# Projecting the keys' latent, v and part of c_q as seven products of halved matrices

## The chip, the cores and the metric

One core of a Trainium2 chip runs the whole kernel as one program. The metric is the device time of one execution in microseconds (us), median of several runs. The engines are named as in the profile: PE is TensorE's matrix multiply and PEld its weight load, DVE is VectorE, ACT is ScalarE, POOL is GpSimd, and SP is SyncE, which here only issues DMA transfers, in the order of its queue.

## The reference

One layer of a decoder, 1024 tokens of 1024 features in float32: a feed-forward half step, a mixer with three branches, a second feed-forward half step. The change lies in the mixer's input projection and in what follows it.

```python
h = rmsnorm(x, mix_norm)
z = h @ w_in       # columns: u 512 | v 512 | c_q 384 | c_kv 256 | k_rope 32 | q_mem 512 | gates 3 x 1024
u, v = gelu(z_u), gelu(z_v)
y_a = u * (tril(w_s) @ layernorm(v) + b)                       # 128-token chunks, 8 groups
q  = rope(rmsnorm(rmsnorm(c_q)  @ w_uq))                        # 8 heads of 64 + 32
kv = rmsnorm(c_kv) @ w_ukv                                     # 8 heads of 64 + 64
k  = rope(rmsnorm([kv_nope, k_rope]))
y_b = causal_attention(q, k, kv_v)
y_c = attention(rmsnorm(q_mem), memory of 256 tokens)          # k and v of the memory from mem_w_kv
x  = x + (sum_i sigmoid(gate_i) * (y_i @ w_branch_i)) @ w_out
```

## The kernel before

Every operand of a product is kept as two tiles, `hi` (a cast on ACT) and `lo` (the rest, a subtraction on DVE); the function `split` makes both, and `mm3` multiplies with three matmuls per 128 rows of the contraction (hi by hi, hi by lo, lo by hi). So one 128 x 128 block against 512 columns is three matmuls of 512 columns.

Most of the work is done in units of the class `Seven` (feed-forward) and its child `Gates`: a unit makes two 128-feature rows of outputs for all 1024 tokens from four halves of a matrix in seven products of half size, with additions on DVE before and after, as in Strassen's method. A unit is 7 products x 4 blocks x 3 = 84 matmuls of 512 columns. `Gates.run` goes through a list of units (gates, the memory queries, u), in an order of PE written by hand; outputs go to DRAM (`gate0`, `gate1`, ...).

After the last unit comes `mixer`, whose order on the engines is made by a scheduler at build time:

- `latent` projects c_q feature by feature (3 blocks x 2 halves of the tokens x 8 x 3 = 144 matmuls of 512 columns) and c_kv with the rotary key token tile by token tile (`zrow`, 8 tiles x 8 x 3 = 192 matmuls of 288 columns), takes the sums of squares, normalizes c_kv and transposes it.
- `qkv` makes q, k and v of the heads for two token tiles at a time: per tile two banks of 384 columns (9 matmuls each) and one pair of 512 (12 matmuls). ACT copies them out and squares them, DVE sums the squares (L516, L528), takes the inverse roots in a chain of small instructions, and scales q (L541) and k (L543, L545); POOL rotates q (L359 to L364); SP stores v, k and q to DRAM (`vd`, `kd`, `qd`). The tiles q and k have two buffers, v has one.
- `sgu` projects v in `gelu_rows` (192 matmuls of 512 columns), normalizes it (L646 to L652), splits it into v_hi and v_lo, and mixes it over the tokens of a chunk (`mix(0)` and `mix(1)`, one for each half of the tokens: 8 groups of 3 matmuls of 256 columns, eight ACT evictions with a bias into the tile u, 16 transposes of u, four DVE products with the gate u). Among these stands `mem_kv`, keys and values of the memory (two products of 48 matmuls of 512 columns), whose weights come from DRAM as `wkv` (already split).
- then the three branches with their attention.

The pool of `sgu` takes the memory that the pool of `qkv` had.

Of the kernel before, what the change touches and what calls it, by code (L numbers as in the profile page):

```python
# [8 lines left out]
F32 = mybir.dt.float32  # L9
# [32 lines left out]
ZB = ZU + SGW // P  # L42
# [4 lines left out]
class Kernel:  # L47
# [181 lines left out]
    def latent_gains(self, const):  # L229
        nc, a = self.nc, self.a  # L230
        self.g_ckv = self.bcast_row(const, "g_ckv", a["mla_ckv_norm"], KVR)

# [183 lines left out]
    def zrow(self, ps, h, i, w):  # L416

        c = slice(i % 4 * P, i % 4 * P + P)
        for d in range(DT):
            self.mm3(ps, tuple(x[:, c] for x in h[i // 4][d]), w[d], d == 0, d == DT - 1)  # L420

    def to_feature(self, dst, srcs, gain=None):

        nc = self.nc
        b = self.bank()
# [9 lines left out]
    def latent(self, h):  # L435
# [4 lines left out]
        cq = [self.split_pair() for _ in range(QR // P)]  # L440
        ckv = [self.split_pair() for _ in range(KVR // P)]
        kr, krs, krr, eps = (self.lp.tile(s, F32, name=n) for s, n in (
            ([P, NT, ROPE], "kr"), ([P, NT], "krs"), ([P, NT, ROPE], "krr"), ([P, NT], "eps")))
        w = self.convert(self.w_cq)

        def c_q(hf):
            acc, cols = None, slice(hf * 512, hf * 512 + 512)
            for j, d in enumerate(cq):
                b = self.bank()
                for k in range(DT):  # L450
                    self.mm3(b, w[j * DT + k], h[hf][k], k == 0, k == DT - 1)
                acc = self.norm_feed(acc, b, 512)
                self.split_gain(d[0][:, cols], d[1][:, cols], b, self.g_cq[:, j:j + 1])
            nc.vector.tensor_scalar(
                eps[:, hf * 4:hf * 4 + 4], self.token_sums(acc), EPS / QR, EPS * EPS, op0=ALU.mult, op1=ALU.add)

        n, width = a["w_ckv"].shape[-1], KVR
        with tc.tile_pool(name="lat", bufs=1) as p:
            wkv = self.load(
                a["w_ckv"], lambda: [p.tile([P, 3 * n], F32R, name=x, bufs=3) for x in ("kvhi", "kvlo")])  # L460
            for hf in (1, 0):
                c_q(hf)
                xs = []
                for j in range(2):
                    pm = self.mm() if j == 0 else None
                    ss = self.stat("l_ss", 2)
                    for k in range(2):
                        i = hf * 4 + j * 2 + k
                        ps = pm[:, k] if pm is not None else self.bank()
                        self.zrow(ps[:, :n], h, i, wkv)  # L470
                        x = p.tile([P, n], F32, name="l_xs", bufs=6)
                        sq = p.tile([P, n], BF16, name="l_junk", bufs=2)
                        nc.scalar.activation(sq[:, :width], ps[:, :width], ACT.Square, accum_out=ss[:, k:k + 1])
                        nc.scalar.copy(x, ps[:, :n])
                        nc.scalar.activation(sq[:, width:], x[:, width:], ACT.Square, accum_out=krs[:, i:i + 1])
                        nc.scalar.copy(kr[:, i], x[:, width:])
                        xs.append(x)
                    r = self.rms(ss, 2, width)
                    for k, x in enumerate(xs[-2:]):
                        nc.vector.scalar_tensor_tensor(  # L480
                            x[:, :width], in0=x[:, :width], scalar=r[:, k:k + 1], in1=self.g_ckv,
# [1588 lines left out]
```

## Time and profile before

| what | value |
|---|---|
| median of 3 runs | 2186.36 us (2186.1 to 2187.63) |
| profiled execution | 2187.86 us, its span 2186.1 us |
| granted clock over the span | 0.998 |
| PE busy | 2171.8 us, 99% of the span |
| DVE, ACT, POOL busy | 1559.3, 907.0, 268.9 us |

The span is the time from the first to the last instruction that the profiler saw. A busy PE is one with a matmul in flight: the engine can be busy without a pause and still run a matmul slowly if its clock is lowered. The granted clock says how far it was: 1.00 is 2.4 GHz and 0.50 is 1.2 GHz.

### The profile page before, as it was taken

How to read it: one execution, taken by the hardware profiler on the slowest of the kernel's cores; microseconds unless marked ns; L12 is line 12 of the kernel's file. 1: busy time of each engine (PE TensorE's matmuls, PEld its weight loads, DVE VectorE, ACT ScalarE, POOL GpSimd, SP SyncE). 2: the span in 40 equal slices, each digit the busy share in tenths (PEclk: the TensorE clock that was granted, in tenths of full speed). 3: DMA queues.
4: the chain of work that ended last, by engine and by line, in shares of the span. 5: the costliest groups of instructions: out<-in, count | busy, mean ns of one | idle time of the engine just before them, and what ended most of it. 6: DMA issues, size and time to landing. Idle time of an engine off the chain costs nothing.

```text
span 2186.1 us, 27650 instructions
## 1 busy us (share of the span) xinstructions
PE 2171.8 (99%) x10258; PEld 1813.6 (83%) x10258; DVE 1559.3 (71%) x2384; ACT 907.0 (41%) x1490; POOL 268.9 (12%) x269
## 2 busy tenths in 40 slices
PE   9999999999999999999999999999999999999999
PEld 5888888888887888889888889988888888888887
DVE  7976666679889656653876679885886666667884
ACT  5433333343445434443535469833432322234332
POOL 3011111100000000000311321140011211210000
PEclk9999999999999999999999999999999999999999
DMA  4253444385433444532495631093033223337443
GB/s 146 83 192 140 145 140 154 137 316 173 130 116 105 146 167 168 176 108 73 161 311 198 247 144 59 14 355 133 30 141 97 98 98 101 116 124 295 169 130 106
DMA packets 123927, 324.72 MB, mean 149 GB/s; under 512 B 14608, under 2 KB 22928, under 8 KB 123792
## 3 DMA queue, kind: packets, MB, share of 16 engines
q1 hardware_dynamic: 123792, 322.96, 42.3%
q8 instruction: 80, 1.31, 0.2%
q14 instruction: 55, 0.45, 0.1%
HBM read 221.72 MB, written 101.19 MB: 148 GB/s over the span
## 4 chain that ended last, share of the span: by engine, by line
PE 92%; DVE 4%; ACT 1%; DMA 1%; issue 1%; POOL 1%; SPq 0%; ACTq 0%; POOLq 0%
PE one L148 14%; PE one L150 14%; PE one L149 14%; PE bank L148 13%; PE bank L149 13%; PE bank L150 13%; PE mm L148 2%; PE mm L149 2%; PE mm L150 2%; PE bank L989 1%; PE bank L1004 1%; DMA w<-in_ffn_w_gu_dram 1%; PE bank L1005 1%; PE bank L428 1%; DVE wlo L137 1%
## 5 line engine op out<-in xcount | busy, mean ns | idle before, releaser
L136 ACT CAST whi<-x 128x1024 fp32r<-128x1024 f32 (+1 forms) x201 | 191.4, 954 | 443.8 <-PE one L149 168.7
L1390 DVE TENSOR_TENSOR t<-t,one 128x512 f32<-128x512 f32 x186 | 127.7, 687 | 214.6 <-PE one L150 214.5
L137 DVE TENSOR_TENSOR wlo<-x,whi 128x1024 fp32r<-128x1024 f32 (+1 forms) x201 | 243.5, 1213 | 34.3 <-ACT whi L136 24.7
L148 PE MATMUL bank<-h,whi 128*128 128x512 f32 x676 | 263.4, 390 | 0.0
L149 PE MATMUL bank<-h,whi 128*128 128x512 f32 x676 | 263.1, 389 | 0.0
L150 PE MATMUL bank<-h,wlo 128*128 128x512 f32 x676 | 263.0, 389 | 0.0
L148 PE MATMUL one<-h,whi 128*128 128x512 f32 x508 | 199.6, 393 | 0.0
L149 PE MATMUL one<-h,whi 128*128 128x512 f32 x508 | 198.4, 391 | 0.0
L150 PE MATMUL one<-h,wlo 128*128 128x512 f32 x508 | 198.4, 391 | 0.0
L148 PE MATMUL one<-w,whi 128*128 128x512 f32 x424 | 165.4, 390 | 0.1
L150 PE MATMUL one<-w,wlo 128*128 128x512 f32 x424 | 165.0, 389 | 0.0
L149 PE MATMUL one<-w,whi 128*128 128x512 f32 x424 | 165.0, 389 | 0.0
L1812 POOL TENSOR_TENSOR raw<-raw 128x512 f32<-128x512 f32 x38 | 57.0, 1501 | 800.3 <-DVE raw L1667 713.7
L131 ACT CAST whi<-w 128x1024 fp32r<-128x1024 f32 (+1 forms) x108 | 95.1, 899 | 143.4 <-PE one L149 55.2
L132 DVE TENSOR_TENSOR wlo<-w,whi 128x1024 fp32r<-128x1024 f32 (+1 forms) x108 | 110.1, 1033 | 60.8 <-ACT whi L131 60.7
L150 PEld LDWEIGHTS bank<-h,wlo 128*128 128x128 f32 x676 | 126.9, 188 | 26.4
L149 PEld LDWEIGHTS bank<-h,whi 128*128 128x128 f32 x676 | 126.9, 188 | 26.2
L148 PEld LDWEIGHTS bank<-h,whi 128*128 128x128 f32 x676 | 126.9, 188 | 26.0
L148 PE MATMUL bank<-whi 128*128 128x512 f32 x352 | 136.9, 389 | 0.0
L149 PE MATMUL bank<-wlo,whi 128*128 128x512 f32 x352 | 136.9, 389 | 0.0
L150 PE MATMUL bank<-whi,wlo 128*128 128x512 f32 x352 | 136.9, 389 | 0.0
L149 PEld LDWEIGHTS one<-h,whi 128*128 128x128 f32 x508 | 96.0, 189 | 20.0 <-issue 0.2
(391 smaller groups left out, 4895.6 us busy)
## 6 DMA issues: line engine op xcount, KB each, us to landing
x<-in_ffn_w_gu_dram SPq DMA_DIRECT2D x78, 512.0 KB, 4.9
w<-tdt SPq DMA_DIRECT2D x40, 512.0 KB, 4.3
tdb<-raw SPq DMA_DIRECT2D x64, 256.0 KB, 2.1
h<-in_ffn_w_down_dram SPq DMA_DIRECT2D x64, 256.0 KB, 6.0
gate<-raw SPq DMA_DIRECT2D x31, 512.0 KB, 2.8
w<-tdb SPq DMA_DIRECT2D x30, 512.0 KB, 4.7
tdt<-w SPq DMA_DIRECT2D x48, 256.0 KB, 2.1
x<-in_w_gate_dram SPq DMA_DIRECT2D x21, 512.0 KB, 6.4
```

The lines of the kernel that those rows point to most:

```text
L131: self.nc.scalar.copy(hi, src)
L132: return (eng or self.nc.vector).tensor_tensor(lo, src, hi.bitcast(F32), op=ALU.subtract)
L136: self.nc.scalar.copy(hi, src)
L137: return lambda: self.nc.vector.tensor_tensor(lo, src, hi.bitcast(F32), op=ALU.subtract)
L148: i = mmul(out, s[0], m[0], start=first, stop=False, **kw)
L149: mmul(out, s[0], m[1], start=False, stop=False, **kw)
L150: self.last = mmul(out, s[1], m[0], start=False, stop=last, **kw)
L428: nc.tensor.transpose(b[:m, k * P:(k + 1) * P], s, self.ident)
L989: nc.tensor.transpose(b[:, at:at + P], prs[t][:, kk * P:(kk + 1) * P], self.ident)
L1004: nc.tensor.matmul(o, w, pt[0], start=n == 0, stop=False)
L1390: return self.nc.vector.tensor_tensor(out, x, y, op=ALU.add)
L1812: sub = lambda d, x, y: (eng or nc.gpsimd).tensor_tensor(d, x, y, op=ALU.subtract)
```

## The change

One unit more is put among the gates' units (`ZC // 2`, ninth in the list). It makes 256 of the 384 columns of c_q and stores them as `gate32` and `gate33`; `parts` splits them with their gain into the DRAM tensor `cq`, and `latent_squares` and `latent_sums` make the sums of squares. The remaining 128 columns of c_q, c_kv, the rotary key and v (416 + 512 = 928 columns) are projected in `token_rows`, which stands behind the last unit in the same hand-written order of PE. Both the 928 columns and the 1024 tokens and the 1024 features are halved, and the 2 x 2 x 2 blocks are multiplied in seven products; the tokens' combinations are those that the units already had (`norm.op`), and those of the weights are made by `both` on DVE. A product is 4 token tiles x 4 blocks of the contraction x 3 = 48 matmuls of 464 columns, so there are 336.

`latent`, `zrow` and `gelu_rows` fall away, and with them the second loading and normalization of a half of x that `Gates.run` did for them. The new class `Latents` normalizes c_kv (`norm`), loads the c_q of DRAM back (`load`), and transposes c_kv and the last 128 columns of c_q (`turn`). v's layer normalization moves: for the first half of the tokens it stands in `qkv`, as `asides` between the pairs of token tiles; for the second half it stands behind `mem_kv`'s first product. `sgu` begins with the splits of v and `mem_kv`; half of the first product's weights are loaded ahead, into tiles of the x4 pool.

```diff
@@ run
-            r0 = self.const.tile([P, 4], F32, name="r0")
-            gates.run(x1d, r0)
+            latents = gates.run()
...
-            merged = self.mixer(norm)
+            merged = self.mixer(latents)
@@ Gates.run
-        units = [3, 4, ZQ // 2, 5, 6, ZQ // 2 + 1, *range(7, ZQ // 2), ZU // 2, ZU // 2 + 1]
+        units = [3, 4, ZQ // 2, 5, 6, ZQ // 2 + 1, 7, 8, ZC // 2, *range(9, ZQ // 2), ZU // 2, ZU // 2 + 1]
-                    k.w_cq = list(k.fetch(k.a["w_cq"], [x4, x4]))
-                    for p in range(2):
-                        norm.t.t[0, p] = w4()
-                        self.nc.sync.dma_start(norm.t.t[0, p], x1d[0, p])
-                    norm.s[0] = k.norm_scale(r0)
-                    for p in range(2):
-                        norm.norm(0, p)
+                last = f == units[-1]
+                if last:
+                    self.row_weights(range(5), [w4, x4, x4, x4, x4])
...
+            return self.token_rows()
@@ token_rows
+        def product(out, w, name, first=False, ps=range(2)):
+            for p in ps:
+                for t in range(4):
+                    for i in range(2):
+                        s = tuple(x[:, i, t * P:(t + 1) * P] for x in norm.op[name][p])
+                        k.mm3(out[t][:, :RW], s, w[2 * p + i], first and p + i == 0, p + i == 2, skip_group_check=True)
...
+        product(x, w, "t2", True)
+        w = ready(A12)
+        both(A12, A12, S2, ALU.subtract)
+        v1, _ = room(w4)
+        for t in range(4):
+            tt(v1[t], p1[t], x[t][:, :RW], op=ALU.add)
+        both(A21, A21, A22, ALU.add)
+        product(a, w, "b21")
...
+        product(y, w, "t4", ps=(1,))
+        for t in range(4):
+            tt(v1[t], v1[t], y[t][:, :RW], op=ALU.add)
+            gelu(1, t, v1[t], False)
+        return lat
@@ qkv
                     nc.sync.dma_start(d, q[:, t].rearrange("p (g x) d -> p g (x d)", x=2))
+                next(asides, None)
@@ sgu
-            take(0)
-            mt = self.mem_rows()
-            take(1)
+            split(0)
+            kv = self.mem_kv(self.mem_t, self.mem_w)
+            next(kv)
+            for v in rows[1]:
+                self.layer_norm(v)
+            split(1)
             nc.scalar.activation(self.stat("warm", 1), vs[1][0][:, 3, SGW - 1:].bitcast(F32), ACT.Exp, scale=0.0)
             mix(0)
@@ mixer
-        with tc.tile_pool(name="lt", bufs=1) as self.lp:
-            self.latent_gains(self.lp)
-            self.qkv(*self.latent(h))
+        def asides():
+            lat.turn(0)
+            self.mem_w = self.mem_weights(0, [self.split_pair] * 2)
+            yield
+            self.mem_t = self.mem_rows()
+            self.layer_norm(lat.v[0][0])
+            yield
+            self.layer_norm(lat.v[0][1])
+            yield
```

**PE behind qkv.** Before, the last matmuls of `qkv` (into mm_8566, with halves of the transposed c_kv in x4 tiles) are followed by the first of the 192 for v (into bank_8835 and bank_8836, one bank for each token tile, with the normalized h in h4 tiles):

```order
L148 MATMUL mm_8566<-whi_8098,x4_7460 128x512
L149 MATMUL mm_8566<-wlo_8099,x4_7460 128x512
L150 MATMUL mm_8566<-whi_8098,x4_7461 128x512
L148 MATMUL bank_8835<-whi_8637,h4_5214 128x512
L148 MATMUL bank_8836<-whi_8637,h4_5214 128x512
L149 MATMUL bank_8835<-wlo_8638,h4_5214 128x512
```

Now `qkv` ends with mm_8795, and `mem_kv`'s first product begins (mm_8878), with weights that were loaded ahead (x4_8400, x4_8401) and the memory's rows (h4_8536, h4_8537):

```order
L151 MATMUL mm_8795<-whi_8242,h4_8114 128x512
L152 MATMUL mm_8795<-wlo_8243,h4_8114 128x512
L153 MATMUL mm_8795<-whi_8242,h4_8115 128x512
L151 MATMUL mm_8878<-x4_8400,h4_8536 128x512
L152 MATMUL mm_8878<-x4_8401,h4_8536 128x512
L153 MATMUL mm_8878<-x4_8400,h4_8537 128x512
```

When `mem_kv`'s 96 matmuls are through (the last of them into mm_9119), the first of `mix(0)` follow, which need v_hi_8860 and v_lo_8861:

```order
L151 MATMUL mm_9119<-whi_8964,h4_8538 128x512
L152 MATMUL mm_9119<-wlo_8965,h4_8538 128x512
L153 MATMUL mm_9119<-whi_8964,h4_8539 128x512
L151 MATMUL bank_9033<-v_hi_8860,x4_8856 128x256
L151 MATMUL bank_9038<-v_hi_8860,x4_8856 128x256
L151 MATMUL bank_9043<-v_hi_8860,x4_8856 128x256
L151 MATMUL bank_9048<-v_hi_8860,x4_8856 128x256
```

The matmuls of v have gone from behind `qkv`, and `mix(0)`, between whose groups matmuls of `mem_kv` stood before, now stands behind the last of these by itself.

**ACT behind qkv.** Now, behind `qkv`'s last evictions (L462 to L464) and those of `mem_kv`'s first product (L624, L625), the casts of v for both halves come (h_7967 and h_7968 are the first), then the load of an activation table (L603), and then the eight evictions of `mix(0)` (L587):

```order
L624 ACTIVATE t<-mm 128x512
L625 COPY h_8927<-mm 128x512
L624 ACTIVATE t<-mm 128x512
L625 COPY h_8927<-mm 128x512
L134 CAST whi<-raw 128x512 x4
L134 CAST v_hi<-h_7967 128x1024
L134 CAST v_hi<-h_7968 128x1024
L134 CAST v_hi<-h_7794 128x1024
L134 CAST v_hi<-h_7795 128x1024
L603 ACT_TABLE_LOAD
L603 ACTIVATE warm<-v_hi 128x1
L587 ACTIVATE u<-bank,c_sg_b 128x4x64 x8
```

Before, the order behind `qkv`'s last evictions was the Gelu of the first half of v (L610) and two casts:

```order
L525 ACTIVATE sq<-mm 128x512
L526 COPY k<-mm 128x8x64
L527 COPY v<-mm 128x512
L610 ACTIVATE x_8669<-mm 128x1024
L610 ACTIVATE x_8670<-mm 128x1024
L131 CAST v_hi<-x_8669 128x1024
L131 CAST v_hi<-x_8670 128x1024
L610 ACTIVATE h_8833<-bank 128x512 x2
L610 ACTIVATE h_8834<-bank 128x512 x2
```

The first two casts write tiles that lie in memory of the pool of `qkv`, and in the new order they wait for the stores of its last k and q (`kd`, `qd`).

**DVE at the beginning of qkv.** Before, the sums of squares (tile qk_ss) followed the last subtraction for the transposed c_kv at once:

```order
L132 TENSOR_TENSOR x_7459<-bank,x_7458 128x512
L132 TENSOR_TENSOR x_7461<-bank,x_7460 128x512
L516 TENSOR_REDUCE qk_ss<-sq 128x8
L534 TENSOR_SCALAR qk_v<-qk_ss,eps 128x8
L528 TENSOR_REDUCE qk_ss<-sq 128x8
L529 TENSOR_SCALAR qk_ss<-qk_ss,krs 128x8
```

Now statistics and first steps of v's normalization (L551, L552, L555; h_7794 and h_7795 are rows of v) and subtractions for weights stand among the first of them:

```order
L135 TENSOR_TENSOR wlo<-raw,whi 128x512 x2
L551 BN_STATS bn<-h_7794 128x6
L551 BN_STATS bn<-h_7795 128x6
L552 BN_AGGR mv<-bn 128x2
L551 BN_STATS bn<-h_7795 128x6
L453 TENSOR_REDUCE qk_ss<-sq 128x8
L552 BN_AGGR mv<-bn 128x2 x2
L555 SCALAR_TENSOR_TENSOR h_7794<-h_7794,mv,h_8139 128x512
L552 BN_AGGR mv<-bn 128x2
```

The scheduler has moved the normalization of the first rows of v ahead of the place that the code gives it.

## Rows read from the trace of the kernel before

**Rows 1.** The page: each engine's busy time, share of the span and instructions.

```profile
PE 2171.8 (99%) x10258; PEld 1813.6 (83%) x10258; DVE 1559.3 (71%) x2384; ACT 907.0 (41%) x1490; POOL 268.9 (12%) x269
```

**Rows 2.** PE's waits: who waited for whom, total us, times, longest.

```profile
PE bank L384 <- POOL t L1235: 2.6, 1, 2.6
...
PE bank L148 <- DVE x L132: 1.3, 1, 1.3
```

**Rows 3.** Windows: length, busy time of each engine, clock, DMA share, GB/s.

```profile
840.00:940.00 100.00, 100.00 (x460) 83.30 (x459) 60.38 (x96) 40.76 (x51) 2.96 (x3) 1.00 0.48 163
1020.00:1040.00 20.00, 19.71 (x129) 18.47 (x127) 8.06 (x29) 5.71 (x23) 1.73 (x6) 1.00 0.16 54
1040.00:1050.00 10.00, 9.00 (x48) 8.53 (x49) 6.40 (x15) 8.58 (x20) 0.00 (x0) 1.00 0.05 21
1041.00:1098.00 57.00, 57.00 (x279) 50.81 (x280) 48.88 (x94) 30.05 (x65) 20.68 (x20) 1.00 0.55 184
1087.00:1150.00 63.00, 63.00 (x301) 52.86 (x300) 46.50 (x121) 20.48 (x36) 8.69 (x9) 1.00 0.91 310
1150.00:1160.00 10.00, 9.54 (x66) 8.56 (x64) 7.56 (x12) 7.55 (x15) 0.00 (x0) 1.00 0.86 331
```

**Rows 4.** Timeline of PE: start, length, instruction, at three places.

```profile
985.55 0.30 PE L148 MATMUL mm<-kvhi,h 128*128 128x288 f32 x1
...
989.52 0.29 PE L148 MATMUL mm<-kvhi,h 128*128 128x288 f32 x1
...
1050.14 0.33 PE L148 MATMUL bank<-whi,x 128*128 128x384 f32 x1
...
1053.28 0.39 PE L148 MATMUL mm<-whi,x 128*128 128x512 f32 x1
...
1085.56 0.39 PE L148 MATMUL mm<-whi,h 128*128 128x512 f32 x1
...
1087.15 0.39 PE L148 MATMUL bank<-whi,h 128*128 128x512 f32 x1
```

**Rows 5.** Groups of DVE by shape, 1041 to 1160: busy us, mean ns.

```profile
L132 DVE TENSOR_TENSOR wlo<-raw,whi 128x512 fp32r<-128x512 f32 x12 | 10.0, 860 | 0.0
...
L671 DVE TENSOR_TENSOR t<-t,bank 128x512 f32<-128x512 f32 x8 | 5.1, 681 | 1.4 <-PE bank L670 1.4
...
L646 DVE BATCH_NORM_STATS2 bn<-x 128x6 f32<-128x512 f32 x4 | 2.6, 686 | 8.4 <-ACT x L610 8.4
```

**Rows 6.** Timelines of DVE, SP and ACT: the end of qkv, and v.

```profile
1094.08 1.76 DVE L541 TENSOR_TENSOR q<-q,rs_y 128x1536 f32<-128x1536 f32 x1
...
1101.67 1.10 SPq L553 DMA_DIRECT2D qd<-q  x2
...
1118.80 2.74 DVE L652 SCALAR_TENSOR_TENSOR x<-x,rs_y,ln_b 128x512 f32<-128x512 f32 x4
...
1120.37 1.06 ACT L131 CAST v_hi<-x 128x1024 fp32r<-128x1024 f32 x1 [12.50 <-DMA wlo<-wkv]
```

**Rows 7.** DMA issues, 1040 to 1180: times, KB each, median us to landing.

```profile
qd<-q SPq DMA_DIRECT2D x8, 384.0 KB, 3.5
...
h<-mrows SPq DMA_DIRECT2D x4, 512.0 KB, 7.0
```

**Rows 8.** Timelines of PE and ACT and ACT's groups: transposes of k, mix(1).

```profile
1149.64 1.03 PE L428 MATMUL bank<-ident,h 128*128 128x128 f32 x8
1150.43 0.36 PE L148 MATMUL bank<-v_hi,x 128*128 128x256 f32 x1
...
1156.58 0.48 PE L148 MATMUL bank<-x,whi 128*128 128x512 f32 x1
...
1152.33 3.05 ACT L664 ACTIVATE u<-bank,c_sg_b 128x256 f32<-128x256 f32 x8
...
L677 ACT ACT_TABLE_LOAD x1 | 1.3, 1283 | 0.0
```

**Rows 9.** Window behind PE's longest wait, columns as in rows 3.

```profile
39.00:46.00 7.00, 6.95 (x23) 5.84 (x24) 5.22 (x15) 1.04 (x1) 0.00 (x0) 0.55 0.00 0
```

More of the change, by code (lines that the diff above doesn't have):

```diff
@@ L413, in norm_put, with to_feature @@
         self.split(hi, lo, x)
[L416 to L422, printed above, removed]
+    def to_feature(self, dst, srcs, gain=None, bank=None):
         nc = self.nc
-        b = self.bank()
+        b = (bank or self.bank)()
         m = srcs[0].shape[-1]
@@ L433, in to_feature, with qkv @@
             self.split_gain(dst[0], dst[1], v, gain)
-    def latent(self, h):
+    def qkv(self, lat, asides):
         nc, a, tc = self.nc, self.a, self.tc
         half = ROPE // 2
[L440 to L481, printed above, removed]
-                            op0=ALU.mult, op1=ALU.mult)
-                for c, d in enumerate(ckv):
-                    self.to_feature(
-                        tuple(t[:, hf * 512:hf * 512 + 512] for t in d),
-                        [x[:, c * P:(c + 1) * P] for x in xs])
-                t = slice(hf * 4, hf * 4 + 4)
-                self.rotate(
-                    nc.gpsimd, p, krr[:, t], kr[:, t], [x[:, t] for x in self.rope["k"]], [P, NT // 2, half])
-        return cq, ckv, krr, krs, eps
@@ L492, in qkv @@
-    def qkv(self, cq, ckv, krr, krs, eps):
-        nc, a, tc = self.nc, self.a, self.tc
-        half = ROPE // 2
+        cq, krr, krs, eps = lat.cq, lat.krr, lat.krs, lat.eps
         wq = self.load(a["mla_w_uq"])
@@ L785, in query_roots, with latent_squares, latent_sums @@
         nc.gpsimd.tensor_scalar(self.mq_nr[:, :, c], self.mq_r[:, :, c], -1.0, None, op0=ALU.mult)
+    def latent_squares(self, z):
+        return self.squares([[(slice(0, P), z[ZC + n])] for n in range(2)])
+    def latent_sums(self, t):
+        self.cq_s = self.const.tile([P, NT], F32, name="cq_s")
+        self.nc.vector.tensor_copy(self.cq_s, self.token_sums(t))
     def mem_rows(self):
@@ L832, in mem_kv, with mem_weights @@
         self.split(vv[0], vv[1], ps)
-        return kt, vv
+        yield kt, vv
+    def mem_weights(self, g, rooms, c0=0):
+        out = []
+        for c, room in enumerate(rooms):
+            ts = room() if room else (self.wide("whi"), self.wide("wlo"))
+            for t, src in zip(ts, self.wkv[g, c0 + c]):
+                self.nc.sync.dma_start(t.bitcast(F32), src)
+            out += [tuple(t[:, i * 512:i * 512 + 512] for t in ts) for i in range(2)]
+        return out
     def mem_queries(self, pair, rooms):
@@ L1639, in run, with row_weights @@
                     sums[n](got.pop())
+                if last:
+                    for _ in range(2):
+                        next(steps)
+                    self.row_weights(range(5, 8), [w4, w4, x4])
                 for _ in steps:
                     pass
-            for p in range(2):
-                norm.put("b12", p, norm.t.t[0, p])
+            return self.token_rows()
+    def row_weights(self, ns, rooms):
+        for n, room in zip(ns, rooms):
+            t = room().rearrange("p a w -> p (a w)")[:, :2 * RW]
+            self.nc.sync.dma_start(t, self.k.a["w_rows"][n // 2, n % 2])
+            self.rw[n] = t
```

235 lines of the change are left out of this document (165 added, 70 removed).

## The prediction

> **What bounds the kernel now.** I read the page first: PE is busy for 99% of the span [rows 1], so the time is the sum of PE's instructions plus what little PE waits. Next I read PE's waits, because only those can be won back: the longest is 2.6 us, at the start of the kernel, and the third row is 1.3 us where `qkv` begins [rows 2]. The windows say where in the region of this change PE is not busy: 20.00 - 19.71 = 0.29 us, 10.00 - 9.00 = 1.00 us and 10.00 - 9.54 = 0.46 us, together 1.75 us; between 1041 and 1150 there is none [rows 3]. So the kernel is bound by the columns that PE streams, and two questions decide the change: how many columns fewer, and whether PE still finds its operands ready.
>
> **What a matmul costs.** The price is the distance between starts, since the listed length overlaps the next one. From the timeline [rows 4]: 288 columns, 30 matmuls from 985.55 to 989.52, 0.132 us; 384 columns, 18 from 1050.14 to 1053.28, 0.174 us; 512 columns, 7 from 1085.56 to 1087.15, 0.227 us. No row has 464 columns. It lies between 0.174 and 0.227, and since the three prices lie nearly on a line (0.44 and 0.41 ns per column), I take 0.174 + 80 x 0.00041 = 0.207 us; the line's bend moves it by less than 0.001, or 0.3 us over all.
>
> **PE's sum.** Removed: c_q's 144 x 0.227 = 32.7, c_kv's 192 x 0.132 = 25.4 and v's 192 x 0.227 = 43.6 us, together 101.7. Added: the unit's 84 x 0.227 = 19.1 and 336 x 0.207 = 69.6 us, together 88.7. Transposes: four for the scale of the reloaded half go, eight for the last columns of c_q come; eight take 0.8 us (1149.64 to 1150.43 [rows 8]), so 0.4 more. Net: 88.7 + 0.4 - 101.7 = -12.6 us of PE.
>
> The Trainium skill, page "TensorE: Matmul & The Clock Gate", section "Back-to-back issue gap", gives an isolated gap of N/2.4 + 2.5 ns at full clock. That would be 216 ns for 512 columns where this trace has 227. With the page's prices (216, 122, 196) the same sum is 84.0 + 0.4 - 96.0 = -11.6 us, so what is priced by the page hardly differs; the trace decides.
>
> **What hides.** The extra unit lies among units where PE is busy for 100.00 of 100.00 us, DVE for 60.38 and ACT for 40.76 [rows 3]; its additions and evictions are of the kinds already there, and cost nothing as long as DVE has that slack (without it, up to its share of DVE). In `token_rows` a product lasts 48 x 0.207 = 9.9 us. Its densest round on DVE is two subtractions for lo and four sums of weights at 928 columns, at 1.76 us for 1536 columns [rows 6] some 1.06 us each, and four sums from PSUM at 464 columns, at 0.68 for 512 [rows 5] some 0.62: 6.4 + 2.5 = 8.9 us. It fits with 1.0 us to spare, so I set this to 0; the upper bound is about 1 us in each of the two or three dense products.
>
> **What PE will wait for.** v was more than work: its 43.6 us stood between `qkv` and the mixing, and behind it the tail of `qkv` drained unseen. Four places:
>
> 1. *Entry of qkv.* Before it cost 1.0 us, a subtraction on DVE behind the transposes (1.3 in rows 2). The same transposes' subtractions are there, so 1.0 again; bounds 0 and 1.3.
>
> 2. *Inside qkv.* DVE is busy for 48.88 of the 57.00 us from 1041 to 1098 [rows 3]. It loses the lo parts of w_v, 8 x 0.86 = 6.9 us [rows 5]; it gains the normalization of half of v, 2.6 us of statistics [rows 5], 2.74 us for four instructions [rows 6] and as much for the four before them, and I estimate 2 us for the small ones, together 10.1; and three subtractions for the transposes that moved here, 2.0. That is +5.2 us. The new order also puts several of them ahead of the first sum of squares, some 3 us, most of which DVE's 8.1 us of idle time pays back; I add 0.9. Of these 6.1 us PE feels a part at once, since q has two tiles and PSUM few banks: I put 2.2 there and 3.9 into the lag at the end. Bounds: 0 and 6.1.
>
> 3. *Before mix(0).* v_hi is cast into memory of `qkv`'s pool, so it waits until the last q has been stored. In the trace the last product of `qkv` gives way to v at 1087.15 [rows 4], the last scaling of q ends at 1094.08 + 1.76 = 1095.8, its rotated copy is issued at 1101.67 and the second issue ends 1.1 later [rows 6], and a `qd` store lands 3.5 us after its issue (median) [rows 7]. So 8.7 + 3.9 lag = 12.6, + 7.0 to the end of the issue, + 3.5, + two casts of 1.06 [rows 6] = 25.2 us behind `qkv`'s last matmul. PE has only `mem_kv` meanwhile, 96 x 0.227 = 21.8. Wait: 3.4 us. Bounds: without the added lag it is 21.3, so 0; with a landing of 7.0 us, as `mrows` had in the same stretch where the DMA share is 0.91 [rows 7, 3], and all 6.1 of lag, 3.4 + 3.5 + 2.2 = 9.1.
>
> 4. *The two mixes.* In the trace `mix(0)` was spread between matmuls of `mem_kv`; now it stands alone. ACT has two more casts (2.1), the table load (1.3) and eight evictions in 3.05 us [rows 8]: 6.5. Then the last transposes, 0.4, and three products on DVE of 0.68 [rows 5] before `mix(1)` has a bank: 8.9. `mix(1)` takes 1156.58 - 1150.43 = 6.15 [rows 8], as it did. Together 15.1 us, for work of about 2 x 5.2 + 0.8 = 11.2 (of the 6.15, 0.46 was idle and about 0.5 another product's). Wait: 3.9 us; bounds 1 and 6.
>
> **The sum.** Waits 1.0 + 2.2 + 3.4 + 3.9 = 10.5 us, in place of 1.75: +8.75. With -12.6 that is -3.9 us on the profiled execution of 2187.86, 2184.0 us. That execution lies 1.5 us above the median 2186.36, so against the runs I say 2182.5. A difference under about 0.2%, 4.4 us, can't be told from none here.
>
> **Rivals.**
> - *The stalls stay hidden; most of the 12.6 us arrives.* DVE's 8.1 idle us swallow the normalization and the store lands in time: waits 2 and 3 vanish, and the time is 2182.5 - 5.6 = 2177; if the mixes wait only 1 us each, 2175. For it: 21.3 against 21.8 us without the added lag. Against it: the first sum of squares starts late, and a lag on DVE at the end of `qkv` is there already.
> - *Slower: the wait before mix(0) grows and takes the clock with it.* In the trace the longest wait of PE, 2.6 us [rows 2], is followed by 7.00 us at a granted clock of 0.55, that is half of 2.4 GHz for most of it [rows 9]: 7.00 x 0.45 = 3.15 us of work not done. The wait before `mix(0)` is forecast longer, and if the clock falls with it, 2182.5 + 3.1 = 2185.6; with the wait at its bound of 9.1, 5.7 more, 2191. It decides from a wait of about 8.5 us on (5.1 over mine), where the time is 2190.7 and the change is slower by over 0.2%. Against it: where PE waits for ACT anyway in `mix(0)`, a slow matmul costs less than on a full PE, and a landing of 7.0 is twice the median of `qd`.
> - *DMA is the bound after qkv.* `mem_kv`'s weights come as ten transfers of 0.5 MB once `qkv`'s weights let go of their tiles; at 310 GB/s [rows 3] 5.2 MB are 17 us and must be there within 20 or so. It would be 2 to 4 us, 2184.5 to 2186.5: no change.
>
> The Trainium skill warns, on the same page, section "HAM oscillation — how this bites in real kernels", that idle gaps of PE between bursts send the clock back to its low level. The start of this trace agrees with it [rows 9]; it is the second rival's mechanism.
>
> **How the numbers follow.** Forecast with waits of 8 to 13 us (2180 to 2186): 0.43. Hidden stalls (2174 to 2180): 0.27. Long wait with a lower clock (2186 to 2194): 0.15, of which 0.11 lies over 2190.7. Several waits at their upper bounds together, the dense products of `token_rows` among them (2191 to 2198): 0.12. Late weights: 0.03. The range from 2175 to 2193 leaves out the end of the second case and half of the last but one, under 2 in 10; the likeliest case's own range is 2179 to 2187. Faster by over 0.2% (below 2182.0): the 0.27 and a little over a third of the first case, 0.43. Slower (above 2190.7): 0.11 and 0.12, 0.23. The same: 0.34.
>
> **What would show it.** Right: the same distance of 0.207 us in `token_rows`, without idle time of PE there; PE idle for about 3 us before the first matmul on v_hi, released by the store of q; the eight evictions of `mix(0)` pacing PE; PE's busy time lower by about 13 us. Wrong: a first sum of squares in `qkv` that isn't late, a store that lands before `mem_kv` ends, or PE waiting inside `token_rows` for a subtraction on DVE, which would mean that my round of 8.9 us was too short. A granted clock near 0.5 after the wait would speak for the second rival.

## The result, and the profile after

The median of 11 runs is 2191.66 us (2190.79 to 2193.41) against 2186.45 us (11 runs) before: a ratio of 1.0023, interval 1.0014 to 1.0032. The changed kernel is 0.24% slower; 2182.5 was predicted. The profiled execution took 2190.79 us, 2.9 more than that of before, which lay above its median while this one lies below its own.

The page first, each engine's busy time:

```profile
span 2189.1 us, 27495 instructions
PE 2164.3 (99%) x10154; PEld 1806.3 (83%) x10154; DVE 1583.6 (72%) x2389; ACT 915.2 (42%) x1500; POOL 275.4 (13%) x274
```

PE is busy 7.5 us less than in [rows 1], though its slowed matmuls (below) are in that sum; the work did become less. PE's waits tell where it went (of the region of the change alone; those elsewhere are much as before):

```profile
PE bank L151 <- ACT v_hi L134: 7.0, 1, 7.0
...
PE mm L151 <- DMA whi<-wkv: 1.8, 1, 1.8
...
PE bank L151 <- ACT u L587: 1.4, 3, 0.9
PE mm L151 <- ACT v L464: 1.1, 1, 1.1
```

Where [rows 2] had 1.3 us in this region, one wait of 7.0 us now stands before `mix(0)`, and one of 1.8 in `mem_kv`. The windows place them (columns as in [rows 3]):

```profile
1060.00:1080.00 20.00, 19.91 (x107) 18.07 (x106) 18.18 (x38) 13.11 (x27) 5.30 (x12) 1.00 0.59 211
1100.00:1110.00 10.00, 8.86 (x43) 7.82 (x44) 7.93 (x30) 8.07 (x19) 0.74 (x2) 1.00 0.71 229
1110.00:1120.00 10.00, 10.00 (x46) 8.29 (x45) 9.63 (x17) 1.67 (x4) 6.46 (x6) 1.00 1.02 399
1120.00:1130.00 10.00, 9.14 (x41) 7.23 (x39) 9.81 (x16) 4.13 (x8) 6.78 (x6) 1.00 1.06 373
1130.00:1140.00 10.00, 4.60 (x12) 3.35 (x12) 6.10 (x33) 0.00 (x0) 0.00 (x0) 0.76 1.05 385
1140.00:1150.00 10.00, 6.94 (x34) 6.38 (x35) 5.05 (x5) 8.74 (x14) 0.00 (x0) 0.56 0.03 7
```

The last three columns are the reading. From 1110 to 1140 the DMA engines are busy without a pause at 370 to 400 GB/s; from 1130 to 1140 ACT and POOL do nothing and PE half; then the transfers stop (0.03) and ACT starts. The granted clock falls to 0.76 and 0.56. PE's timeline shows both stretches:

```profile
1109.71 0.39 PE L153 MATMUL mm<-whi,h 128*128 128x512 f32 x1
1109.94 0.39 PE L151 MATMUL mm<-x,h 128*128 128x512 f32 x1
...
1130.98 0.50 PE L151 MATMUL mm<-whi,h 128*128 128x512 f32 x1 [1.84 <-DMA whi<-wkv]
...
1131.82 0.63 PE L151 MATMUL mm<-whi,h 128*128 128x512 f32 x1
1132.24 0.63 PE L152 MATMUL mm<-wlo,h 128*128 128x512 f32 x1
...
1142.59 1.20 PE L151 MATMUL bank<-v_hi,x 128*128 128x256 f32 x4 [7.01 <-ACT v_hi L134]
...
1158.28 0.48 PE L151 MATMUL bank<-x,whi 128*128 128x512 f32 x1
```

`qkv` ends at 1109.71 and `mem_kv` begins at 1109.94. Behind the wait for weights the distance of two matmuls is 0.42 us in place of 0.23: half clock. `mix(0)` begins at 1142.59, and the branches at 1158.28, 1.7 us later than in [rows 8]. This execution had won 1.6 us in its first 90 us, ahead of the change: the same matmul stands at 691.28 before and at 689.70 now. From there the branches come 468.6 us later, before 465.3: the change cost 3.3 us up to here. What `mix(0)` waited for is a chain over four engines, in the timelines of DVE, POOL, SP and ACT:

```profile
1120.81 1.76 DVE L478 TENSOR_TENSOR q<-q,rs_y 128x1536 f32<-128x1536 f32 x1
...
1128.42 1.17 POOL L363 TENSOR_TENSOR q<-rot,rot 128x256 f32<-128x256 f32 x1
...
1124.42 2.33 SPq L590 DMA_DIRECT2D t<-gate  x4
...
1129.40 1.93 SPq L590 DMA_DIRECT2D t<-gate  x2
1131.65 0.33 SPq L100 DMA_DIRECT2D raw<-in_w_branch_dram  x1
1132.32 1.02 SPq L490 DMA_DIRECT2D qd<-q  x2
...
1140.50 3.89 ACT L134 CAST v_hi<-h 128x1024 fp32r<-128x1024 f32 x4 [15.36 <-DMA raw<-in_w_branch_dram]
```

The last q is scaled at 1122.57 and rotated at 1129.59. SP issues its store only at 1132.32, behind loads for the mixes and the branches. The casts begin at 1140.50, 7.2 us after the end of that issue and 0.2 us after the second half of the store has landed (1140.28). The releaser in brackets is the transfer that came last by the profile, another one. The landing times of 1100 to 1150 (median, last column; the first in [rows 7] was 3.5):

```profile
whi<-wkv SPq DMA_DIRECT2D x6, 512.0 KB, 8.1
...
qd<-q SPq DMA_DIRECT2D x6, 384.0 KB, 7.1
...
t<-gate SPq DMA_DIRECT2D x6, 256.0 KB, 7.0
```

The 3.5 is a median of eight stores. The last two of these, the pair of the last q, took twice as long before the change too (its view of the tile qd, 1101 to 1103):

```profile
DMA to landing us min/median/max: 7.6/7.7/7.9
```

### The profile page after: what moved, and what is told of

Same layout as the page of the kernel before. It is cut to its first block, busy times and chain, and to the rows that moved or that the text cites. A ratio compares the mean times of both kernels' runs of the same rounds, so it can differ in the third digit from the quotient of the medians.

```text
span 2189.1 us, 27495 instructions
## 1 busy us (share of the span) xinstructions
PE 2164.3 (99%) x10154; PEld 1806.3 (83%) x10154; DVE 1583.6 (72%) x2389; ACT 915.2 (42%) x1500; POOL 275.4 (13%) x274
## 4 chain that ended last, share of the span: by engine, by line
PE 90%; DVE 5%; ACT 2%; DMA 1%; issue 1%; POOL 1%; SPq 0%; ACTq 0%; POOLq 0%; DVEq 0%
PE one L151 15%; PE one L152 15%; PE one L153 15%; PE bank L151 13%; PE bank L152 12%; PE bank L153 12%; PE bank L926 1%; PE mm L151 1%; PE mm L152 1%; PE mm L153 1%; PE bank L941 1%; PE bank L942 1%; PE bank L421 1%; DVE wlo L140 1%; DMA kd<-k 0%
## 5 line engine op out<-in xcount | busy, mean ns | idle before, releaser
L151 PE MATMUL bank<-h,whi 128*128 128x512 f32 x636 | 247.7, 390 | 0.0
L153 PE MATMUL bank<-h,wlo 128*128 128x512 f32 x636 | 247.5, 389 | 0.0
L152 PE MATMUL bank<-h,whi 128*128 128x512 f32 x636 | 247.4, 389 | 0.0
L151 PE MATMUL one<-h,whi 128*128 128x512 f32 x516 | 202.4, 392 | 0.0
L152 PE MATMUL one<-h,whi 128*128 128x512 f32 x516 | 201.2, 390 | 0.0
L151 PE MATMUL one<-w,whi 128*128 128x512 f32 x432 | 168.7, 391 | 0.0
L152 PE MATMUL one<-w,whi 128*128 128x512 f32 x432 | 168.1, 389 | 0.0
L135 DVE TENSOR_TENSOR wlo<-w,whi 128x1024 fp32r<-128x1024 f32 (+2 forms) x113 | 115.8, 1038 | 69.9 <-ACT whi L134 69.6
L134 ACT CAST whi<-w 128x1024 fp32r<-128x1024 f32 (+2 forms) x113 | 100.0, 902 | 152.9 <-PE one L152 63.3
L153 PEld LDWEIGHTS bank<-h,wlo 128*128 128x128 f32 x636 | 119.4, 188 | 24.9
L151 PEld LDWEIGHTS bank<-h,whi 128*128 128x128 f32 x636 | 119.4, 188 | 24.7
L152 PEld LDWEIGHTS bank<-h,whi 128*128 128x128 f32 x636 | 119.4, 188 | 24.5
```

Source lines behind the costliest of these rows:

```text
L134: self.nc.scalar.copy(hi, src)
L135: return (eng or self.nc.vector).tensor_tensor(lo, src, hi.bitcast(F32), op=ALU.subtract)
L151: i = mmul(out, s[0], m[0], start=first, stop=False, **kw)
L152: mmul(out, s[0], m[1], start=False, stop=False, **kw)
L153: self.last = mmul(out, s[1], m[0], start=False, stop=last, **kw)
```

## The experiments

The theory: v's 43.6 us had covered the tail of `qkv` and the loads behind it. Without that cover the last q's store decides when `mix(0)` starts, and it is late by its place in SP's queue and because the transfers saturate DMA. Rivals: the lag on DVE is the cause; the low clock is; the order on ACT (all four casts and a table load ahead of `mix(0)`'s evictions) is; the mixes' own pace is.

All medians are of 11 runs (r1_late and r5_cover of 5). Runs on one chip vary by 1 or 2 us, and the median of the kernel before lies between 2186.45 and 2187.48 on the chips used; the ratio is to before on the same chip, and is the better guide. The table gives a length of the profile too, from the first matmul of 464 columns to the first of the branches (170.56 us in the changed kernel: 987.72 to 1158.28), and PE's wait for v_hi or v_lo of the first half. The length is 785 or 786 matmuls long, but r2_own, r1_late, r12_less, r9_order and r8_kv have 4 to 24 in it that stand behind it elsewhere. In r2_own, r7_best and r9_order four matmuls on v_hi have no record, so about 0.5 us of their wait is work.

| kernel | median us | ratio to before, interval | length | wait |
|---|---|---|---|---|
| the change | 2191.66 | 1.0023 (1.0014 to 1.0032) | 170.56 | 7.0 |
| r1_late | 2196.25 | 1.0039 (1.0026 to 1.0053) | 175.22 | 8.7 |
| r2_own | 2190.46 | 1.0015 (1.0006 to 1.0024) | 168.39 | 0.5 |
| r3_nonorm | 2188.27 | 1.0004 (0.9996 to 1.0013) | 167.64 | 5.3 |
| r4_half | 2187.13 | 1.0001 (0.9992 to 1.0010) | 164.70 | 5.4 |
| r5_cover | 2200.52 | 1.0060 (1.0046 to 1.0074) | 179.18 | none |
| r6_store | 2186.54 | 0.9998 (0.9989 to 1.0007) | 166.05 | 3.5 |
| r7_best | 2185.14 | 0.9991 (0.9983 to 1.0000) | 163.95 | 2.0 |
| r8_kv | 2191.48 | 1.0018 (1.0009 to 1.0027) | 171.77 | 3.3 |
| r9_order | 2184.31 | 0.9987 (0.9979 to 0.9996) | 164.64 | 0.8 |
| r10_norm_store | 2186.74 | 0.9999 (0.9990 to 1.0007) | 164.16 | 2.4 |
| r11_warm | 2191.52 | 1.0022 (1.0013 to 1.0031) | 172.56 | 1.6 |
| r12_less | 2185.24 | 0.9988 (0.9979 to 0.9997) | 164.38 | none |

**r5_cover: the cover given back.** 96 matmuls of 512 columns that nobody needs, between `qkv` and `mem_kv`.

```diff
             split(0)
+            b = self.mm()
+            for n in range(96):
+                nc.tensor.matmul(b[:, n % 2], self.mem_w[0][0][:, :P], self.mem_w[0][0], start=True, stop=True)
             kv = self.mem_kv(self.mem_t, self.mem_w)
```

> 96 matmuls of 512 columns on data at hand, whose results nobody reads, stand on PE between qkv's last matmul and mem_kv's first: 21.8 us of work added, half of what v's products were there before the change. If the waits and the low clock behind qkv come from the cover that v's products gave, they go: 7.0 for v_hi, 1.8 for weights, and about 4 us of low clock, so the time rises by 9 to 11 us only, 2200 to 2203. If they have another cause (the order on DVE or ACT, the memory as such), the waits move along and the time is 2211 to 2214.

The time rose by 8.9 us (8.6 against before on its chip) for 96 x 0.227 = 21.8 us of work added, as the first theory said. The other 13 are waits and slow matmuls that are no longer there:

```profile
1105.00:1135.00 30.00, 30.00 (x138) 25.32 (x138) 21.23 (x49) 7.87 (x17) 12.01 (x12) 1.00 0.96 340
1135.00:1160.00 25.00, 25.00 (x129) 21.32 (x128) 15.29 (x47) 12.63 (x22) 0.00 (x0) 1.00 0.57 193
```

PE is busy in 55.00 of 55.00 us at a clock of 1.00. So the loss lies between `qkv` and the branches, and time to hide in removes it. The build also put groups of `mix(0)` between `mem_kv`'s matmuls again (1145.63 and 1153.66), so not all of the 13 us is due to the added time alone; which link needed the time is for the others to tell.

**r1_late and r8_kv: other orders.** r1_late puts the second half's casts and the table load behind `mix(0)`'s evictions on ACT; r8_kv puts `mem_kv`'s second product ahead of `mix(0)` in the code.

```diff
+                    c = nc.scalar.copy(hi, v)
+                    if hf:
+                        self.after(c, self.last_u)
...
+            mix(0)
             split(1)
             nc.scalar.activation(self.stat("warm", 1), ...)
-            mix(0)
```

```diff
+            kv = next(kv)
             mix(0)
...
-            kv = next(kv)
```

> Only the order behind qkv is changed: the casts of v's second half and the table load stand behind mix(0)'s eight evictions on ACT, no longer ahead of them. All theories expect PE's wait for v_hi to stay at about 7 us, since what v_hi waits for is the same. If the order on ACT costs what its rows say (two casts 2.1 us and a table load 1.3 us ahead of the first eviction), mix(0) ends up to 3 us earlier: about 2189 to 2190. If PE at its low clock sets the pace of mix(0) anyway, nothing moves: 2191.7.

> Only the code's order is changed: mem_kv's second half stands ahead of mix(0), so that the scheduler can put matmuls of the memory's attention between the groups of mix(0), as matmuls of mem_kv stood there before the change. The wait for v_hi stays at about 7 us in all theories. If the bare mixes cost what the prediction put on them (3.9 us), 2188 to 2190; if the wait and the clock are all, 2191 to 2192.

r1_late is 4.6 us slower than the change (3.8 against before on each chip), a miss: the wait for v_hi stays (8.7), and what came off ACT ahead of `mix(0)` returns ahead of `mix(1)`, as 1.9 us for u, 1.0 for the memory's keys on ACT and 0.75 for v_lo. r8_kv gives the time of the change, as its second case said; of the wait, 4.5 us go to the memory's keys and 3.3 stay before v_hi. An order alone moves the wait; v_hi is late in all of them.

**r2_own: no wait for the store.** The first half's v_hi, v_lo and u get memory that the last pair's k and q don't use, on top of r1_late's order.

```diff
+        self.v_own = vp.__enter__().tile([P, 4, SGW], F32R, name="v_own")
...
-                vs[hf] = v8("v_hi"), v8("v_lo")
+                vs[hf] = (v8("v_hi"), v8("v_lo")) if hf else (self.v_own, lo8())
```

> As the run with the order alone, but v_hi and v_lo of the first half and u lie in memory that the last pair's q and k never had, so mix(0) no longer waits for the last store (q and k of alternate pairs lie in two pools; v of the heads lies in another pool's tiles). Theory of the memory: the wait for v_hi of 7.0 us goes; what is left before mix(0) is the subtraction for v_lo on DVE, 1 to 3 us, and the second half's v waits ahead of mix(1), 0 to 3 us; the low clock is shorter: 2183 to 2186. Rival, that DVE or the weights of mem_kv hold PE as much: 2188 or more.

The wait before `mix(0)` is 0.5 us, so it was that memory and the store. But only 1.2 us of the median come back (2.0 against before on each chip), as the rival said:

```profile
PE bank L151 <- ACT v_hi L578: 4.4, 1, 4.4
PE mm L151 <- DMA whi<-wkv: 3.6, 1, 3.6
```

ACT reaches the second half's casts at 1145.74, behind other work without a pause, 1.6 us after the last store has landed (1144.16): it is their place on ACT behind `mix(0)`'s evictions that PE waits for. `mem_kv`'s weights come later than in the change. One wait was exchanged for two.

**r3_nonorm, r4_half, r6_store: three links apart.** r3_nonorm leaves out the normalization of v's first half (the lag on DVE). r4_half loads 3.1 MB less (six lo tiles of `mem_kv`'s weights; hi tiles stand in). r6_store leaves nothing out: SP takes the last q's store ahead of the loads of u's gates and of the branches' weights.

```diff
-            self.layer_norm(lat.v[0][0])
             yield
-            self.layer_norm(lat.v[0][1])
             yield
```

```diff
-            ts = room() if room else (self.wide("whi"), self.wide("wlo"))
-            for t, src in zip(ts, self.wkv[g, c0 + c]):
+            ts = room() if room else (self.wide("whi"),) * 2
+            for t, src in zip(ts if room else ts[:1], self.wkv[g, c0 + c]):
```

```diff
+            if self.loads is not None:
+                self.loads += 1
+                if 3 < self.loads < 8:
+                    self.after(i, self.behind)
...
-                    nc.sync.dma_start(d, q[:, t].rearrange("p (g x) d -> p g (x d)", x=2))
+                    self.behind = nc.sync.dma_start(d, q[:, t].rearrange("p (g x) d -> p g (x d)", x=2))
...
-                    nc.sync.dma_start(u, self.z[ZU + j][:, hf])
+                    self.after(nc.sync.dma_start(u, self.z[ZU + j][:, hf]), self.behind)
```

> The normalization of v's first half is left out (10 us of DVE in qkv). Theory of the lag on DVE: the last scaling of q ends about 8.7 us behind the last matmul of qkv, not 12.6, the last store starts 4 to 6 us earlier, and the wait for v_hi of 7.0 us shrinks to 1 to 3: 2184 to 2187. Rival, that the transfers queued ahead of the store set its landing: the wait stays at 5 us or more, 2189 to 2191.

> Of mem_kv's weights that come behind qkv, the lo tiles are not loaded (the hi tile is used in their place), so 3.1 MB of 6.3 MB fall away, about 8 us at the 385 GB/s of that stretch; matmuls stay the same in number. Theory of the transfers: the wait for weights of 1.8 us goes, the last store of q lands in 3 to 4 us, not 7.2, is issued 1 to 3 us earlier, and the wait for v_hi shrinks to 2 to 4 us: 2184 to 2187. Rival, that DVE's lag alone sets the store: the wait for v_hi stays above 5.5 us, 2189 to 2190 (the 1.8 us alone).

> Only the order on SP is changed: the loads of the gate u for the mixes and the later loads of the first branch's weights (about 2 to 2.6 MB) stand behind the store of the last q, not ahead of it. Theory of the transfers: at 385 GB/s 5 to 7 us fewer are queued ahead of that store, it is issued at the end of POOL's rotation and lands 4 to 7 us earlier, and the wait for v_hi of 7.0 us shrinks to 0 to 3: 2184 to 2188. Theory of the lag alone (DVE and POOL set the store): it starts 2.7 us earlier and no more is gained, the wait stays above 4: 2188 to 2190.

Timelines of SP and ACT, with the store and the first casts; r3_nonorm first:

```profile
1129.82 1.89 SPq L490 DMA_DIRECT2D qd<-q  x2
...
1138.40 3.89 ACT L134 CAST v_hi<-h 128x1024 fp32r<-128x1024 f32 x4 [9.91 <-DMA qd<-q]
```

r4_half:

```profile
1130.38 0.92 SPq L490 DMA_DIRECT2D qd<-q  x2
...
1135.95 3.89 ACT L134 CAST v_hi<-h 128x1024 fp32r<-128x1024 f32 x4 [10.06 <-DVE h L557]
```

r6_store:

```profile
1130.44 0.91 SPq L496 DMA_DIRECT2D qd<-q  x2
1131.40 3.87 SPq L597 DMA_DIRECT2D t<-gate  x6
...
1136.04 3.89 ACT L140 CAST v_hi<-h 128x1024 fp32r<-128x1024 f32 x4 [10.09 <-DMA t<-gate]
```

What SP waited for at its issues of q's stores, from SP's waits of 1120 to 1140 (us in total, times, longest), in the change, r3_nonorm, r4_half and r6_store:

```profile
SPq L490 <- DMA t<-gate: 0.5, 2, 0.3
SPq L490 <- DMA whi<-wkv: 1.1, 1, 1.1
SPq L490 <- POOL q L363: 1.2, 1, 1.2
SPq L496 <- POOL q L369: 5.3, 2, 3.3
```

In the change and in r3_nonorm the last wait is for an earlier transfer, in the other two for POOL's q. The traces show why. SP's transfers use eight semaphores in turn, and at no issue are more than seven earlier ones still to land: each issue waits until the transfer eight places ahead has landed. For the store this was at 1132.25 in the change (issue at 1132.32) and at 1129.76 in r3_nonorm (issue at 1129.82), where the rotation had ended at 1124.83 already. In r4_half and r6_store the rotation ends at 1130.4 and the store is issued at once.

These profiles reach the region 0.7 to 0.9 us later than the change's, so I count from the first matmul of 464 columns. The casts begin 152.8 us behind it in the change, 150.0 in r3_nonorm, and 147.4 in both r4_half and r6_store, each 0.2 to 0.3 us after the second half of the store has landed. Fewer bytes or another place in the queue do the same thing. Against before on the same chip r4_half and r6_store are 0.1 us faster, so each gives back the whole loss of 5.2; r3_nonorm stays 1.0 slower, so the lag on DVE is worth some 4 of the 5.2 by itself. The three don't add up, since each shortens one chain. Of the expectations only r6_store's first held in its time; its wait of 3.5 lies above that theory's 0 to 3. r3_nonorm has the rival's wait (5.3) but a time between the two, and r4_half's time is 0.1 us above its first range with a wait of 5.4, between the two.

**r10_norm_store and r12_less: links together.** r10_norm_store is r6_store without the normalization of v's first half; r12_less leaves out r4_half's bytes as well.

> Leaves out the normalization of v's first half, and puts the last q's store ahead of the loads for the mixes on SP. Alone, the first gave 3.4 us and the second 5.1 us against the changed kernel. If the lag on DVE and the place in SP's queue are two links of one chain, q's store is issued some 4.5 us earlier than with the queue alone, near 1126, the wait for v_hi (3.5 us there) is gone, and the time is 2182 to 2184.5. Rival: with the store early, the weights of mem_kv come late instead, PE waits 3 us or more for them, and the time stays at 2186 to 2187.

> Leaves out the normalization of v's first half and 3.1 MB of transfers behind qkv (mem_kv's weights are multiplied with hi tiles in place of the lo tiles that aren't loaded); SP takes the last q's store ahead of the loads for the mixes. If the saturated transfers are what kept the shorter chain on DVE from paying, the store lands within 5 us of its issue near 1127, the wait for v_hi (2.4 us with the transfers) and that for weights are gone, and the time is 2181.5 to 2184.5. Rival: the mixes' own pace (ACT's evictions, DVE's products) decides by now, and the time stays at 2185.5 to 2187.

r10_norm_store missed by 2.2 us: by the ratio it is no better than r6_store. Counted as above, its store is issued 4.7 us earlier than there, but the two issues take 3.59 us, and the casts begin at the same time, 147.3 us against 147.4:

```profile
1127.20 3.59 SPq L496 DMA_DIRECT2D qd<-q  x2
...
1137.40 3.89 ACT L140 CAST v_hi<-h 128x1024 fp32r<-128x1024 f32 x4 [7.04 <-DMA t<-gate]
```

Its windows:

```profile
1130.00:1140.00 10.00, 7.58 (x36) 6.06 (x34) 8.60 (x34) 2.96 (x4) 0.00 (x0) 1.00 1.05 366
1140.00:1150.00 10.00, 6.98 (x53) 6.13 (x52) 7.70 (x11) 9.56 (x19) 0.00 (x0) 1.00 0.65 246
```

DMA is full (1.05) until 1140, and the store takes 8.8 us to land, since it joins transfers that are already waiting: 3072 KB, 1280 in r6_store. The time is the rival's, though PE no longer waits for weights. r12_less takes the bytes away (timelines of SP and ACT, then a window):

```profile
1126.36 1.05 SPq L496 DMA_DIRECT2D qd<-q  x2
...
1132.28 2.00 ACT L140 CAST v_hi<-h 128x1024 fp32r<-128x1024 f32 x2 [2.24 <-DMA t<-gate]
```

```profile
1140.00:1150.00 10.00, 6.75 (x41) 5.70 (x42) 10.00 (x14) 9.84 (x20) 0.00 (x0) 0.91 0.88 296
```

The casts begin at 1132.28 (142.6 us, counted as above) and the waits for v_hi and for weights are gone, as the theory said; but the time, 2185.24, falls between the two expectations. Two things take the place: a wait of 2.8 us for ACT's copy of v where `mem_kv` begins (2.7 in r10_norm_store), and the mixes, which last 17.5 us from 1136.59 to 1154.09 with DVE busy for 10.00 and ACT for 9.84 of 10 us. The second half's normalization and casts and eight more matmuls now lie among them. Once v_hi is early, these two engines are full, so by their shares they are the bound; no run tests it.

**r11_warm: the clock.** 28 matmuls that nobody needs, 6.4 us, behind `mem_kv`'s last and so inside the wait of 7.0.

```diff
+        b = self.mm()
+        for n in range(28):
+            i = nc.tensor.matmul(b[:, n % 2], w[-1][0][:, :P], w[-1][0], start=True, stop=True)
+            if n == 0:
+                self.after(i, self.last)
+        for m in self.first:
+            self.after(m, i)
```

> Adds work that nobody needs: 28 matmuls of 512 columns (28 x 0.227 = 6.4 us) behind mem_kv's last matmul, inside PE's wait of 7.0 us for v_hi. If the low clock behind that wait costs time, mix(0) now runs at full clock and the time falls by 1 to 2.4 us, to 2189 to 2190.5, in spite of the added work. Rival: mix(0) is paced by ACT's evictions and by the transposes' chain, a slow matmul there costs nothing, and the time stays at 2191 to 2192.5.

The time stays, as the rival said, but the test is weaker than meant: `mix(0)` began at full clock, and then the clock fell all the same, behind short waits in it (r11_warm's windows):

```profile
1143.70:1147.50 3.80, 2.36 (x13) 1.89 (x13) 3.65 (x4) 3.77 (x6) 0.00 (x0) 0.77 0.00 0
1147.50:1150.00 2.50, 2.50 (x12) 2.50 (x12) 0.00 (x0) 2.17 (x6) 0.00 (x0) 0.50 0.00 0
```

So it doesn't price the clock. Six runs have the same 88 or 89 matmuls in the mixes. r10_norm_store's are at a clock of 1.00 and take 14.8 us (1139.49 to 1154.27). At 0.79 to 0.83 they take 15.2 (r4_half), 15.6 (r3_nonorm), 15.7 (the change), 16.5 (r6_store) and 16.9 us (r11_warm). So the low clock goes with 0.4 to 2.1 us more, 0.9 in the change; the runs differ in other things too, so this is an estimate. It is not what made the change slower: r6_store's mixes run at 0.79, and its time is that of before.

**r7_best and r9_order: a faster version.** r7_best has r1_late's order, r2_own's memory, r6_store's queue and one more pair of `mem_kv`'s weights loaded ahead. r9_order adds an order on DVE: the branches' first weights and the second half's normalization behind v_lo of the first half.

```diff
-            self.mem_w = self.mem_weights(0, [self.split_pair] * 2)
+            self.mem_w = self.mem_weights(0, [self.split_pair] * 2 + [ahead])
```

```diff
-                self.split(hi[:, c], lo[:, c], raw[:, c], self.nc.gpsimd if at in pool else None)
+                i = self.split(hi[:, c], lo[:, c], raw[:, c], self.nc.gpsimd if at in pool else None)
+                if self.late is not None:
+                    self.after(i, self.late)
...
-        self.nc.vector.tensor_scalar(v, ss, 1.0 / width, EPS, op0=ALU.mult, op1=ALU.add)
+        i = self.nc.vector.tensor_scalar(v, ss, 1.0 / width, EPS, op0=ALU.mult, op1=ALU.add)
+        if self.late is not None:
+            self.after(i, self.late)
```

> Three things together: the order on SP of the run with the store ahead; v_hi, v_lo and u of the first half in memory that the last pair's q and k don't have (v_hi in 8 KB that were free, the others where the pair before and v lay), with the second half's casts behind mix(0)'s evictions; and one more pair of mem_kv's weights (1 MB) loaded ahead into the same 8 KB before v_hi takes them. If memory, transfers and cover are the whole cause, mix(0) follows mem_kv with at most 1 us of wait, mix(1) waits at most 2, the weights are in time and the clock stays up: 2178 to 2182, faster than the kernel before. If something else holds PE (DVE's queue with the normalization of the second half), 2184 to 2189.

> This is the version that has v's first half in memory of its own, the last q's store ahead of other loads and one more pair of weights ahead, with two orders more on DVE: the lo parts of the branches' first weights (3.7 us) and the normalization of v's second half come behind v_lo of the first half. If DVE's order is what is left, v_lo is ready some 3 us earlier, PE's waits of 2.05 and 1.89 us before v_lo fall under 0.5 each, and the time is 2181 to 2183. Rival: PE's next wait is as long (for v_hi of the second half or for the branches' weights, which come later now), and the time stays at 2184.5 to 2186.

r7_best is at 2185.14, in its second case and not at 2178 to 2182. r9_order is at 2184.31: 0.13% under before by the ratio, and the only one that leaves nothing out and has its interval below 1. It missed 2181 to 2183, and it can't be told from r7_best. The wait before v_lo of the first half fell as meant, from 2.0 us (of r7_best) to 0.8; that before v_lo of the second half stayed at 1.9, and one of 1.7 for ACT's u came in (0.4 in r7_best). r9_order's waits:

```profile
PE bank L160 <- DVE v_lo L592: 1.9, 1, 1.9
PE bank L159 <- ACT u L602: 1.7, 1, 1.7
...
PE bank L160 <- issue: 0.8, 1, 0.8
```

## Why the prediction was wrong

The sign and 9.2 us were wrong, in one step mainly: **"Before mix(0)"**, whose terms for the end of the store's issue and for its landing were together 7.5 us too small.

- **PE's sum** (-12.6). 464 columns cost 0.210 us (the matmul at 987.72 and the tenth, at 989.61: 1.89 / 9) where 0.207 was interpolated, 1.0 us more over 336. No wait in `token_rows`, as said (50.00 of 50.00 us busy from 1000 to 1050). As a whole the sum came out: in r5_cover, whose region is at a clock of 1.00, PE is busy for 2182.1 us; less its 21.8 that is 11.5 under the 2171.8 of [rows 1].
- **Entry of qkv** (1.0) was 0.1, 20.00 - 19.91; **inside qkv** (2.2) was 1.1. Both too high, together 2 us to the good, although DVE did more there than was counted: it took the statistics and the first step for all eight rows of v up to 1073.2. The rows h_7794 and h_7795 that the scheduler moved ahead are the second half's; r3_nonorm, without the first half's, still has four of each there.
- **Before mix(0)** is the step that failed. It put the casts' end at 25.2 us behind `qkv`'s last matmul; it was 1142.59 - 1109.71 = 32.9. Term by term: the lag was 12.6 and measured 1122.57 - 1109.71 = 12.9, right, DVE's added work included. From there to the end of the issue I took 7.0 from before; it was 1133.34 - 1122.57 = 10.8: 7.0 for POOL's rotation (5.8 before; why it is slower is open), 2.7 of waiting behind SP's earlier transfers, 1.0 for the issue. For the landing I took the median 3.5 from [rows 7]; from the end of the issue it took 1140.50 - 1133.34 = 7.2. The casts were right. So 3.8 + 3.7 us of the 7.7 lie in two terms. The landing was misread before the change was run: the median mixes six stores at 2.6 to 3.8 us with the last pair, whose own 7.6 and 7.9 were the ones to take; before, nothing waited for them, as v's 43.6 us lay in between. The hold in the queue is new. r6_store and r4_half show that both come from what SP has issued ahead of the store.
- **The waits of 7.0 and 1.8.** PE filled the 32.9 us with 21.8 of `mem_kv`, 1.8 of wait for weights and about 2 of slow matmuls; the rest is the 7.0. Neither the wait for weights nor the clock costs anything of its own there by the trace, as v_hi was later than `mem_kv` anyway and no link of its chain is PE's.
- **The two mixes** (15.1 us) took 1158.28 - 1142.59 = 15.7. The length is right; in part PE filled it by running slowly where idle time was forecast.

The sum by the trace: +1.0 + 7.7 + 0.6 - 0.9 - 1.1 = +7.3 on the predicted -3.9, so +3.4 at the branches; 3.3 was measured from the same matmul. Behind the branches the change loses another 1.3 us (1030.8 against 1029.5 to the end of the span), for which the prediction had nothing. The rest to the 5.2 between the medians lies in how far the two profiled executions stand from theirs.

**The rivals.** "Slower" forecast 2191 for a wait at its bound with a low clock, and the time came out so. That is in part luck: the landing of 7.0 in that bound was right, but the further lag in it did not come, the hold in SP's queue was not in it, and the clock, which did fall, is not what made it slower. "DMA is the bound after qkv" had 0.03. It priced late weights for PE (2 to 4 us; 1.8), which cost nothing by themselves; what the same transfers do to the store that stands among them was in no rival, and it was the cause. From [rows 3] the stretch of v had a DMA share of 0.91 over 63 us; the change has 30 us at 1.02 to 1.06 there, and this was to be seen. The Trainium skill's page "TensorE: Matmul & The Clock Gate", section "HAM oscillation — how this bites in real kernels", says that gaps of PE between bursts bring the low clock; the trace agrees (0.76 and 0.56 above). The runs add that a low clock can cost little where another engine or a store paces PE (r6_store).

Open: the clock's exact price in the mixes, and whether r9_order's remaining waits can be ordered away.

## What to carry to other kernels

Work that is taken off the bounding engine may have been the cover under which stores, loads and a pipeline's tail drained; list everything that was issued in its shadow, in bytes, and see whether it fits into the time that stays. A chain that ends in a store must be priced with the place of its issue in the queue and with the landing time of that very store, not a median over stores in quieter stretches; moving that store ahead of loads that are needed later won back the whole loss here (r6_store). When one wait is removed, look for the next: in r2_own, r9_order and r12_less another engine was late within a few microseconds.

## What was unexpected of the hardware

- How long a `qd` store takes to land goes with what was issued ahead of it on SP's queue and has not landed yet. From 1030 to 1150 SP's transfers land in the order of their issue in all these traces. The first store of a pair took 2.6 to 3.9 us with 896 KB or less ahead, 4.4 to 4.8 with 1280 or 1408 KB (r6_store, r4_half, r12_less), 6.2 to 7.6 with 2304 (6.9 in the change, 7.55 for the last pair before) and 7.8 to 11.3 with 2816 to 3328 (8.8 with 3072 in r10_norm_store). The DMA share tells less: from 1130 to 1136 it is 1.05 in r6_store too.
- An issue itself can stretch: 0.36 and 0.5 us for the last two in r6_store, 0.83 and 2.30 in r10_norm_store.
- The clock fell to half behind a wait of 1.84 us at 1130.98, but not behind one of 1.61 us at the same place in r6_store, nor behind the 1.3 us of [rows 2].
- Putting two of the four casts and a table load behind `mix(0)`'s evictions, which frees ACT for what PE waits for, made the kernel 3.8 to 4.6 us slower (r1_late).
